# GpSimd's constants behind a norm, two transposes moved and the end of attention listed anew, in a two layer decoder trunk

## The chip, the cores and the metric

The kernel runs on one core of a Trainium2 chip. The metric is the device time of one execution in microseconds (us). The engines are TensorE (PE; its weight loads are PEld), VectorE (DVE), ScalarE (ACT), GpSimd (POOL) and SyncE (SP), which here only issues DMAs. They have queues of their own and wait for each other through semaphores.

## What is computed

A trunk of two layers on 512 tokens of 1024 channels, all in float32. Layer 0 mixes tokens by pooling, layer 1 by stick-breaking attention with 16 heads of 64, and each is followed by a squared-ReLU MLP with 4096 hidden channels. Each mixer and each MLP stands between two RMSNorms.

```python
def rms_norm(x, g):
    y = x * lax.rsqrt(jnp.mean(x * x, axis=-1, keepdims=True) + EPS)
    return y * g

for layer in range(2):
    h = rms_norm(x, mix_pre_g[layer])
    if layer < 1:
        m = pool_mixer(h, pool_w[layer], pool_scale[layer])
    else:
        q = jnp.matmul(h, w_q[0]).reshape(B, S, N_HEADS, HEAD_DIM).transpose(0, 2, 1, 3)
        o = stick_breaking_attention(q, k, v)
        m = jnp.matmul(o.transpose(0, 2, 1, 3).reshape(B, S, HD), w_o[0])
    x = x + rms_norm(m, mix_post_g[layer])
    h = rms_norm(x, mlp_pre_g[layer])
    x = x + rms_norm(sq_relu_mlp(h, w_up[layer], w_down[layer]), mlp_post_g[layer])
    if layer == 0:
        kv = jnp.matmul(rms_norm(x, kv_norm_g), w_kv)   # split into k and v, 16 heads each
```

Attention weighs key s for query t (s < t) by sigmoid(z_ts) times the product of 1 - sigmoid(z_tj) over the keys j between them; no softmax is taken.

## The kernel before, in words

Tokens stand in four tiles of 128 (t = 0 to 3), channels in two halves of 512 (n or h = 0, 1) or in eight blocks of 128 (k). For float32 accuracy each operand of a product is split into a rounded high part (a copy on ScalarE) and the rest, the low part (a subtraction on VectorE), and each product is three matmuls: high x high, high x low, low x high (`mm3`, L299, and `up_block`, L691). `up_block` serves the MLP's up projections and attention's key and query projections; with half of the tokens it is 8 x 3 = 24 matmuls of 256 columns.

**What one norm is.** `Update` (L312) carries a tile through "add the normed mixer or MLP output to x, then norm x for the next stage". Its steps, with the letters that the written orders use for them:

- `s`: two ScalarE passes sum the squares of the halves of y into columns of a small tile `stat` (`square_sum`, L284).
- `g`: VectorE multiplies y by the gain row (`product`, L332).
- `V`: GpSimd adds the two sums and eps (`total`, L289) and raises the result to -0.5 (`power`, L296). All totals and powers are on GpSimd, one column each.
- `a`: VectorE adds y times that factor to x (`add_part`, L344).
- `S`: ScalarE sums the squares of the new x. `W`: a second total and power on GpSimd.
- `n`: ScalarE scales x by the new factor (L373), half by half.
- `t`: TensorE transposes a half, four matmuls against a unit matrix (L383). `h` and `l`: ScalarE copies the high part out of PSUM (L393, or L397 where a gain is applied column by column), VectorE takes the low part (L402, L406). Together they write `xnh` and `xnl`, the operands of the next projections.

So V, a, S, W, n, t, h, l is a chain over four engines for each tile, and the four tiles' chains lie side by side.

**What sets the order.** Most of the kernel is ordered by a planner: it simulates the engines and places each instruction in its engine's queue where it expects it to be ready. Inside `tc.manual_schedule(engines=...)` the named engines keep the program's order instead, and other instructions may still be put between. `tc.issue_after(i)` places what a block issues behind instruction i in the same queue, without waiting for its result. The ends of the stages are written out by hand as lists of words.

**Attention's start.** Layer 0's MLP ends in `finish` (L438), whose list `MLP_ORDER[0]` orders TensorE, ScalarE, VectorE and GpSimd by hand up to the norms of tile 3 (n30 n31). The transposes of tiles 2 and 3 are left over as `pending`; `need(t)` (L419) issues them with their high and low parts when something first wants them. Then attention follows `ATT_ORDER` (L59). `V001` is the first value projection (4 heads) for tiles 0 and 1 (`values`, L862; 48 matmuls of 256 columns), `K0` the first half, over tiles 0 and 1, of pair 0's key projection (`start`, L884), `V02` the values of tile 2, `P0` the rest of the key projection and the query projection of pair 0 (`queries_keys`, L910). `S` are scores, sigmoids and the scan of a pair, `T` transposes of its weights, `A` their products with the values, `O` output projections. In before, tile 2's transposes come when V02 asks for them. GpSimd prepares attention's constants where the program opens attention: zeros in the unused halves of `kls` (L908), `begin` (a memset L937 and four selects L942, which mark where a row's scan begins) and single columns of `us` (L948). No order ties them to the norms.

**Attention's end.** `END_ORDER` (L72) lists the last pair's work, the last output projections (`O`, `E`, `F`, `G`, with the matmuls of L300 to L302), the four tiles' norms, and the first four up projections of layer 1's MLP over tiles 0 and 1: `R` loads up weight j, `i` and `k` split it (`high_up`, L1153, on ScalarE; `low_up`, L1157, on VectorE), `u` is its `up_block` (`half_up`, L1159). TensorE, ScalarE, VectorE, GpSimd and SP keep the list's order. The planner may put the MLP's own loads and splits between (L160, L170, L172). At the end of the list in before, VectorE does a20 l10 a21 ev30 k2 g31 g30 a31 a30 k3 l20 l21 l31 l30; ScalarE S20 i2 S21 s30 n20 n21 i3 S31 S30 h20 n31 n30 h21 h31 h30; TensorE u0 u1 t20 t21 u2 t31 t30 u3; GpSimd W2 V3 W3. After that the MLP takes the other half of the tokens (tiles 2 and 3) of the same up projections.

Of the kernel before, what the change touches and what calls it, by code (L numbers as in the profile page):

```python
# [57 lines left out]

ATT_ORDER = [  # L59
    (w[0], int(w[1]), [int(c) for c in w[2:]])  # L60
    for w in """V001 K0 V02 P0 V03 S0 P1 T0 V101 S1 A0 P2 T1 V123 A1 S2 P3 T2 O00123 A2 S3 P4 V201 T3 A3
    S4 P5 T4 V223 S5 A4 P6 V301 T5 S6 A5 V323 P7 T6 E1""".split()
]

# [15 lines left out]
    s21 t10 G31 h10 g21 V2 E30 ev31 a20 s31 F30 l10 S20 G30 a21 i2 u0 ev30 S21 k2 s30 W2 g31 V3 n20 g30  # L80
    u1 n21 a31 i3 a30 S31 k3 t20 S30 t21 h20 u2 W3 n31 l20 n30 h21 t31 t30 h31 l21 u3 h30 l31 l30""".split()
]


# [21 lines left out]
def trunk(ctx, tc, x, consts, grow, pw, wup, wdn, wq, wk, wv, wo, out):  # L106
# [12 lines left out]
    def name(s):  # L119
        uid[0] += 1  # L120
        return f"{s}{uid[0]}"
# [162 lines left out]
    def square_sum(src, junk, st, col):  # L284
        latest["act"] = nc.scalar.activation(junk, src, ACT.Square, scale=D**-0.5, accum_out=st[:, col : col + 1])  # L285

    def total(st, col, eps, op=ALU.add):

        nc.gpsimd.tensor_scalar(  # L289
            out=st[:, col + 2 : col + 3], in0=st[:, col : col + 1], scalar1=st[:, col + 1 : col + 2],  # L290
            scalar2=eps, op0=ALU.add, op1=op,
        )

    def power(st, col):
        r = st[:, col + 3 : col + 4]
        latest["pool"] = nc.gpsimd.tensor_tensor(out=r, in0=st[:, col + 2 : col + 3], in1=mhalf, op=ALU.pow)  # L296
        return r
# [14 lines left out]
    class Update:  # L312
        def __init__(self, t, gpost, scaled, eps=EPS, gpre=None, final=False, xn=None, gcol=None):

            self.t, self.gpost, self.scaled, self.eps = t, gpost, scaled, eps
            self.gpre, self.gcol, self.final = gpre, gcol, final
            self.xn = xn_tile() if xn is None else xn
            self.st = keep.tile([P, 8], F32, tag=f"stat{t}", bufs=4, name=name("stat"))


            self.cuts = NS
            if final and t == T - 1:
                self.cuts, self.scaled = [NS[0], slice(512, 768), slice(768, 1024)], xn_tile()
# [5 lines left out]

        def product(self, n, y):  # L330
            cut = self.cuts[n]
            nc.vector.tensor_tensor(out=self.scaled[:, cut], in0=y, in1=self.gpost[:, cut], op=ALU.mult)  # L332

        def first_rstd(self):
            if len(self.cuts) == 2:
                total(self.st, 0, self.eps)
            else:
                both = self.st[:, 2:3]
                nc.gpsimd.tensor_tensor(out=both, in0=both, in1=self.st[:, 4:5], op=ALU.add)
            self.r = power(self.st, 0)  # L340

        def add_part(self, n):
# [6 lines left out]
            cut = self.cuts[n]  # L349
            square_sum(xt[self.t][:, cut], self.xn[:, cut], self.st, 4 + n)  # L350

        def rstd(self):
            normed_by[self.t] = self
            if self.gpre is None and self.gcol is None:
                total(self.st, 4, EPS)
            else:

                total(self.st, 4, TINY, ALU.max)  # L360
            self.r = power(self.st, 4)

        def homogeneous_eps(self):
# [55 lines left out]
    def need(*tiles):  # L419
        for t in tiles:  # L420
            if t in pending:
                pending.pop(t).transpose()
# [265 lines left out]
        fill(ahead)  # L688
        finish(l, squares[1:], w, y, lambda t, y: update(t, y, gpost))

    def up_block(pu, w, cols):  # L691
        wh = w[0].rearrange("p (k c) -> p k c", k=KC)
        wl = w[1].rearrange("p (k c) -> p k c", k=KC)
        for k in range(KC):
            nc.tensor.matmul(pu[:, cols], wh[:, k, :], xnh[:, k, cols], start=k == 0, stop=False)  # L695
            nc.tensor.matmul(pu[:, cols], wh[:, k, :], xnl[:, k, cols], start=False, stop=False)  # L696
            nc.tensor.matmul(pu[:, cols], wl[:, k, :], xnh[:, k, cols], start=False, stop=k == KC - 1)  # L697


    with tc.tile_pool(name="mix0", bufs=1, reuse_waits="tile") as mp:  # L700
# [158 lines left out]
    with tc.tile_pool(name="att", bufs=1, reuse_waits="tile") as ap:  # L859
        att_pool[0] = ap  # L860

        def values(u, part):  # L862
            if u not in vs:
                w = [get(("v", u, h)) for h in range(2)]
                vs[u] = w, ap.tile([P, T, 4, 2, HD], F32R, tag="v", bufs=2, name=name("v"))
            w, v = vs[u]
            for s in part:
                need(s)
                pv = ps()
                for k in range(KC):  # L870
# [6 lines left out]
                nc.scalar.copy(v[:, s, :, 0, :], pv4)  # L877
                nc.vector.tensor_tensor(
                    out=v[:, s, :, 1, :], in0=pv4, in1=v[:, s, :, 0, :].bitcast(F32), op=ALU.subtract
                )  # L880
# [53 lines left out]


        begin = ap.tile([P, NSEG], mybir.dt.bfloat16, tag="begin", name="begin")
        nc.gpsimd.memset(begin, 0.0)  # L937
        us = [ap.tile([P, NSEG + 1], F32, tag=f"u{a}", name=f"u{a}") for a in range(2)]
        for lo, n in SEG.values():
            c = min(n - P, 1)  # L940
            d = begin[:, lo + n - P - c : lo + n]
            nc.gpsimd.affine_select(  # L942
                out=d, in_=d, pattern=[[-1, P + c]], base=c - 1, channel_multiplier=1,
                compare_op=ALU.not_equal, fill=1.0,
            )
        for at in [lo for lo, n in SEG.values()] + [NSEG]:
            for u in us:
                nc.gpsimd.memset(u[:, at : at + 1], 0.0)  # L948

        class Head:  # L950

# [135 lines left out]
        def end():  # L1087
# [4 lines left out]
            bank, o, ups, up = {}, {}, {}, {}  # L1092

            def projected(key, t, n, pairs, first, stop):
                if first:
# [59 lines left out]
            def low_up(j):  # L1155
                raw, (hi, lo) = up[j]
                latest["dve"] = nc.vector.tensor_tensor(out=lo, in0=raw, in1=hi.bitcast(F32), op=ALU.subtract)  # L1157

            def half_up(j):  # L1159
                early.append((ps(), up[j][1]))  # L1160
                up_block(*early[j], slice(0, S // 2))

            last_heads = heads[last]
            steps = {
# [10 lines left out]
                "g": lambda t, n: ups[t].product(n, y[t][:, NS[n]]),  # L1175
                "V": lambda t: ups[t].first_rstd(), "a": lambda t, n: ups[t].add_part(n),
# [12 lines left out]
            while key not in made:  # L1189
                make()  # L1190

        qk, heads = {}, {}
        for what, i, part in ATT_ORDER:
            if what == "V":
                values(i, part)
            elif what == "K":
                start(("k", i))
            elif what == "P":
                qk[i] = queries_keys(i)
                if i == PAIRS - 1:  # L1200
                    until(("o", 5))
            elif what == "S":
                gate[0] = True
                heads[i] = weights(i)
                fill()
            elif what == "T":
                transposed(heads[i])
                behind.update(latest)
            elif what == "A":
                mix_pair(i, vs[i // 2][1])  # L1210
            elif what == "O" and part:
                out_proj(i, part)
                if i == 0:
                    with tc.issue_after(latest["sp"].ins):
                        gpost1 = gain_row(R_MIX_POST1)
            elif what == "E":
                end()


    with tc.tile_pool(name="mlp1", bufs=1, reuse_waits="tile") as mp:  # L1220
# [55 lines left out]
```

## Time and profile before

| | |
|---|---|
| median of 3 runs | 954.42 us (954.37 to 954.46) |
| the profiled execution | 953.63 us, span 951.9 us, granted clock 0.997 |
| VectorE, ScalarE, GpSimd busy | 707.5, 576.9, 45.5 us |
| DMA | 156.15 MB, mean 164 GB/s |

The span runs from the first to the last instruction of one profiled execution; its own time is somewhat longer. A row of a timeline gives the start in us from the span's start, the length in us, the engine, the line of the kernel, the operation, output<-input and shape, the count, and in brackets how long the engine was idle before and what ended that. Rows of neighbouring equal instructions are merged. The ends of matmuls are modelled, their starts are measured, so times between TensorE's instructions are best taken from start to start. A row of a table by stretch gives the stretch, its length, the busy time of TensorE, its weight loads, VectorE, ScalarE and GpSimd with the number of instructions, the granted clock, the share of the DMA engines and GB/s.

### The profile page before, as it was taken

To read this page: it belongs to the slowest core of one execution; us is meant where nothing else is said; L and a number is where in the kernel's file an instruction comes from. 1 tells how busy PE (TensorE), PEld (TensorE's weight loads), DVE (VectorE), ACT (ScalarE), POOL (GpSimd) and SP (SyncE) were. 2 spreads that over 40 slices of the span, in tenths; PEclk is the share of its full clock that TensorE was granted. 3 is DMA by queue.
4 is the path that set the end of the run, shared out by engine and by line. 5 is a ranking of instruction groups with operands and counts; after the bars stand their busy time and mean duration, and the time that the engine had idled before them with its cause. 6 is when DMAs were issued, how large, how long until landed. Compare 5 with 4: busy or idle time off the path is not lost.

```text
span 951.9 us, 12511 instructions
## 1 busy us (share of the span) xinstructions
PE 940.5 (99%) x4758; PEld 799.6 (84%) x4758; DVE 707.5 (74%) x810; ACT 576.9 (61%) x1015; POOL 45.5 (5%) x88
## 2 busy tenths in 40 slices
PE   9999999999999999999999999999999999999996
PEld 7998888888888888899899988888888888888885
DVE  5875799988979876576577778875595966957856
ACT  6668979788775646456656554775545444444632
POOL 2300000000000014000000001300000000000002
PEclk9999999999999999999999999999999999999998
DMA  8344959789697850522424261432513233133102
GB/s 315 100 167 155 340 213 362 290 285 344 221 322 270 293 176 2 201 91 87 171 94 178 95 259 45 156 126 76 198 37 131 99 133 111 45 133 111 38 8 88
DMA packets 43263, 156.15 MB, mean 164 GB/s; under 512 B 4290, under 2 KB 4674, under 8 KB 43203
## 3 DMA queue, kind: packets, MB, share of 16 engines
q1 hardware_dynamic: 43202, 155.36, 46.3%
q8 instruction: 37, 0.61, 0.3%
q14 instruction: 24, 0.19, 0.1%
HBM read 121.79 MB, written 33.55 MB: 163 GB/s over the span
## 4 chain that ended last, share of the span: by engine, by line
PE 93%; ACT 2%; POOL 1%; DVE 1%; issue 1%; DMA 1%; SPq 0%; POOLq 0%; DVEq 0%; ACTq 0%
PE ps L577 28%; PE ps L697 15%; PE ps L695 15%; PE ps L696 15%; PE ps L300 4%; PE ps L302 4%; PE ps L301 4%; PE ps L1030 2%; PE ps L1013 2%; PE ps L809 1%; PE ps L969 1%; ACT xn L285 1%; PE ps L970 1%; PE ps L383 1%; POOL stat L289 1%
## 5 line engine op out<-in xcount | busy, mean ns | idle before, releaser
L577 PE MATMUL ps<-w,a 128*128 128x512 f32 x1176 | 278.6, 389 | 0.0
L697 PE MATMUL ps<-xnh,w 128*128 128x512 f32 (+1 forms) x712 | 261.5, 368 | 0.1
L696 PE MATMUL ps<-xnl,w 128*128 128x512 f32 (+1 forms) x712 | 261.3, 368 | 0.0
L695 PE MATMUL ps<-xnh,w 128*128 128x512 f32 (+1 forms) x712 | 261.2, 368 | 0.0
L577 PEld LDWEIGHTS ps<-w,a 128*128 128x128 f32 x1176 | 220.6, 188 | 45.9 <-DVE w L282 0.2
L697 PEld LDWEIGHTS ps<-xnh,w 128*128 128x128 f32 x712 | 134.1, 188 | 22.5 <-DVE w L830 0.3
L696 PEld LDWEIGHTS ps<-xnl,w 128*128 128x128 f32 x712 | 134.2, 189 | 21.8
L695 PEld LDWEIGHTS ps<-xnh,w 128*128 128x128 f32 x712 | 133.7, 189 | 22.0
L586 DVE TENSOR_TENSOR y<-ps,y 128x512 f32<-128x512 f32 x124 | 84.4, 687 | 42.7 <-PE ps L577 42.6
L172 DVE TENSOR_TENSOR w<-raw,w 128x1024 fp32r<-128x1024 f32 x58 | 70.9, 1222 | 56.7 <-ACT w L170 56.5
L170 ACT CAST w<-raw 128x1024 fp32r<-128x1024 f32 x58 | 61.0, 1051 | 78.0 <-PE ps L697 77.8
L281 ACT CAST a<-r 128x768 fp32r<-128x768 f32 (+1 forms) x60 | 47.6, 794 | 73.4 <-PE ps L577 54.5
L282 DVE TENSOR_TENSOR a<-r,a 128x768 fp32r<-128x768 f32 (+1 forms) x60 | 54.1, 901 | 12.4 <-ACT a L281 12.2
L281 ACT CAST w<-e 128x1536 fp32r<-128x1536 f32 (+1 forms) x30 | 41.8, 1395 | 26.0 <-DVE e L551 16.6
L994 DVE TENSOR_TENSOR_SCAN e<-u,begin 128x1280 f32<-128x1280 f32 x16 | 45.2, 2822 | 10.9 <-ACT u L978 10.4
L282 DVE TENSOR_TENSOR w<-e,w 128x1536 fp32r<-128x1536 f32 (+1 forms) x30 | 49.4, 1647 | 1.8 <-ACT w L281 1.6
L181 ACT ACTIVATE apart<-apart,eye 128x128 f32<-128x128 f32 (+1 forms) x132 | 43.1, 407 | 0.0
L282 DVE TENSOR_TENSOR w<-w,w 128x1536 fp32r<-128x1536 f32 (+1 forms) x20 | 33.0, 1650 | 7.9 <-ACT w L281 7.9
L609 ACT ACTIVATE r<-ps 128x512 f32<-128x512 f32 x56 | 33.0, 590 | 8.9 <-PE ps L697 8.9
L300 PE MATMUL ps<-w,xnh 128*128 128x256 f32 x128 | 36.5, 286 | 0.9 <-ACT xnh L393 0.9
L282 DVE TENSOR_TENSOR w<-xn,w 128x1536 fp32r<-128x1536 f32 (+1 forms) x20 | 33.0, 1650 | 5.6 <-ACT w L281 5.5
L610 ACT ACTIVATE r<-r 128x512 f32<-128x512 f32 x56 | 35.5, 634 | 1.3
(133 smaller groups left out, 1395.9 us busy)
## 6 DMA issues: line engine op xcount, KB each, us to landing
raw<-in_wup SPq DMA_DIRECT2D x64, 512.0 KB, 4.2
w<-kept SPq DMA_DIRECT2D x60, 512.0 KB, 4.2
kept<-wx SPq DMA_DIRECT2D x30, 512.0 KB, 4.9
w<-in_wdn SPq DMA_DIRECT2D x8, 1536.0 KB, 6.7
kept<-apart SPq DMA_DIRECT2D x24, 512.0 KB, 5.8
xn<-in_wdn SPq DMA_DIRECT2D x8, 1536.0 KB, 8.3
apart<-in_wk SPq DMA_DIRECT2D x7, 512.0 KB, 7.1
apart<-in_wq SPq DMA_DIRECT2D x7, 512.0 KB, 9.3
```

Source lines behind the costliest of these rows:

```text
L170: nc.scalar.copy(hi, raw)
L172: nc.vector.tensor_tensor(out=lo, in0=raw, in1=hi.bitcast(F32), op=ALU.subtract)
L181: nc.scalar.mul(c, c, gc[:, lo + k : lo + k + 1])
L281: latest["act"] = nc.scalar.copy(hi, src)
L282: latest["dve"] = nc.vector.tensor_tensor(out=lo, in0=src, in1=hi.bitcast(F32), op=ALU.subtract)
L300: nc.tensor.matmul(dst, ah, bh, start=start, stop=False)
L577: nc.tensor.matmul(bank, a[:, x, q, TS[t]], w[:, z, q], start=start and q == 0 and k == 0, stop=q == self.n - 1 and k == 2, skip_group_che ...
L586: nc.vector.tensor_tensor(out=part, in0=bank, in1=part, op=ALU.add)
L695: nc.tensor.matmul(pu[:, cols], wh[:, k, :], xnh[:, k, cols], start=k == 0, stop=False)
L696: nc.tensor.matmul(pu[:, cols], wh[:, k, :], xnl[:, k, cols], start=False, stop=False)
L697: nc.tensor.matmul(pu[:, cols], wl[:, k, :], xnh[:, k, cols], start=False, stop=k == KC - 1)
L994: nc.vector.tensor_tensor_scan(out=self.e[:, ::-1], data0=self.u[:, 1:][:, ::-1], data1=begin[:, ::-1], initial=0.0, op0=ALU.mult, op1=ALU ...
```

## The change

1. GpSimd's constants (`kls`, `begin`, `us`) are issued behind the latest power on GpSimd, the one of the last tile's norm.
2. `ATT_ORDER` gets two words: `N2` issues tile 2's transposes ahead of K0, `N3` tile 3's behind it and ahead of V02. TensorE keeps the program's order from V001 to P0.
3. `END_ORDER` from k2 on is listed anew. Tile 2's second total (`wt2`), tile 3's first (`vt3`) and tile 3's second (`wt3`) run on VectorE instead of GpSimd; the powers stay on GpSimd. `H` remembers the latest power, and VectorE's next g, a or k waits until it is done. VectorE's order becomes a20 l10 a21 ev30 wt2 (H) g31 g30 vt3 (H) a31 a30 k2 wt3 l20 k3 (H) l21 l31 l30, where (H) stands at what waits. k2 thus goes from before the products to behind the addition, k3 from before l20 to behind it. The orders of ScalarE and TensorE in the list stay as they were.
4. `up_block` for u2 does the 16 matmuls with the weight's high part first, and then the 8 with its low part.

The number of instructions on TensorE and of DMAs is the same. The rest of the diff moves code into functions.

```diff
 ATT_ORDER
-    V001 K0 V02 P0 V03 S0 P1 ...
+    V001 N2 K0 N3 V02 P0 V03 S0 P1 ...
 END_ORDER
-    ... S20 G30 a21 i2 u0 ev30 S21 k2 s30 W2 g31 V3 n20 g30
-    u1 n21 a31 i3 a30 S31 k3 t20 S30 t21 h20 u2 W3 n31 l20 n30 h21 t31 t30 h31 l21 u3 h30 l31 l30
+    ... S20 G30 a21 i2 u0 ev30 S21 s30 wt2 W2 H g31 g30 vt3 n20 V3 H
+    u1 n21 a31 i3 a30 k2 S31 t20 S30 t21 wt3 W3 H h20 u2 l20 n31 k3 n30 h21 t31 t30 h31 l21 u3 h30 l31 l30
...
-    def total(st, col, eps, op=ALU.add):
-        nc.gpsimd.tensor_scalar(
+    def total(st, col, eps, op=ALU.add, engine=None):
+        (engine or nc.gpsimd).tensor_scalar(
...
-    def up_block(pu, w, cols):
+    def up_block(pu, w, cols, last=False):
+        def low(k):
+            nc.tensor.matmul(pu[:, cols], wl[:, k, :], xnh[:, k, cols], start=False, stop=k == KC - 1)
         for k in range(KC):
             nc.tensor.matmul(pu[:, cols], wh[:, k, :], xnh[:, k, cols], start=k == 0, stop=False)
             nc.tensor.matmul(pu[:, cols], wh[:, k, :], xnl[:, k, cols], start=False, stop=False)
-            nc.tensor.matmul(pu[:, cols], wl[:, k, :], xnh[:, k, cols], start=False, stop=k == KC - 1)
+            if not last:
+                low(k)
+        if last:
+            for k in range(KC):
+                low(k)
...
-        for a in range(2):
-            nc.gpsimd.memset(kls[a][half[1 - a], :].bitcast(F32), 0.0)
+        with tc.issue_after(latest["pool"].ins):
+            for a in range(2):
+                nc.gpsimd.memset(kls[a][half[1 - a], :].bitcast(F32), 0.0)
...
+        with tc.issue_after(latest["pool"].ins):
+            nc.gpsimd.memset(begin, 0.0)
...
+            def hold():
+                held.append(latest["pool"].ins)
+
+            def released(i):
+                if held:
+                    info = mybir.DependencyInfo(mybir.DependencyClass.Sync, mybir.DependencyReason.DATA)
+                    tc.add_manual_dep(i.ins, held.pop().name, info, reason="port")
...
+                "g": lambda t, n: released(ups[t].product(n, y[t][:, NS[n]])), "H": hold,
+                "vt": lambda t: ups[t].first_total(nc.vector), "wt": lambda t: ups[t].second_total(nc.vector),
...
+            elif what == "N":
+                need(i)
...
+        first = [what for what, _, _ in ATT_ORDER].index("P") + 1
+        with tc.manual_schedule(engines={mybir.EngineType.PE}):
+            for x in ATT_ORDER[:first]:
+                step(*x)
+        for x in ATT_ORDER[first:-1]:
+            step(*x)
+        end()
```

More of the change, by code (lines that the diff above doesn't have):

```diff
@@ L60 @@
     (w[0], int(w[1]), [int(c) for c in w[2:]])
-    for w in """V001 K0 V02 P0 V03 S0 P1 T0 V101 S1 A0 P2 T1 V123 A1 S2 P3 T2 O00123 A2 S3 P4 V201 T3 A3
+    for w in """V001 N2 K0 N3 V02 P0 V03 S0 P1 T0 V101 S1 A0 P2 T1 V123 A1 S2 P3 T2 O00123 A2 S3 P4 V201 T3 A3
     S4 P5 T4 V223 S5 A4 P6 V301 T5 S6 A5 V323 P7 T6 E1""".split()
@@ L79 @@
     l01 F20 S10 k1 G20 i0 W1 E21 ev20 R3 n11 k0 s20 F21 t11 h00 g20 G21 R2 E31 h11 l00 ev21 F31 n10 l11
-    s21 t10 G31 h10 g21 V2 E30 ev31 a20 s31 F30 l10 S20 G30 a21 i2 u0 ev30 S21 k2 s30 W2 g31 V3 n20 g30
-    u1 n21 a31 i3 a30 S31 k3 t20 S30 t21 h20 u2 W3 n31 l20 n30 h21 t31 t30 h31 l21 u3 h30 l31 l30""".split()
+    s21 t10 G31 h10 g21 V2 E30 ev31 a20 s31 F30 l10 S20 G30 a21 i2 u0 ev30 S21 s30 wt2 W2 H g31 g30 vt3 n20 V3 H
+    u1 n21 a31 i3 a30 k2 S31 t20 S30 t21 wt3 W3 H h20 u2 l20 n31 k3 n30 h21 t31 t30 h31 l21 u3 h30 l31 l30""".split()
 ]
@@ L331, in product, with first_total @@
             cut = self.cuts[n]
-            nc.vector.tensor_tensor(out=self.scaled[:, cut], in0=y, in1=self.gpost[:, cut], op=ALU.mult)
+            return nc.vector.tensor_tensor(out=self.scaled[:, cut], in0=y, in1=self.gpost[:, cut], op=ALU.mult)
+        def first_total(self, engine=None):
+            total(self.st, 0, self.eps, engine=engine)
+            self.summed = True
         def first_rstd(self):
             if len(self.cuts) == 2:
-                total(self.st, 0, self.eps)
+                if not self.summed:
+                    self.first_total()
             else:
@@ L350, in squares_of_x, with second_total @@
             square_sum(xt[self.t][:, cut], self.xn[:, cut], self.st, 4 + n)
+        def second_total(self, engine=None):
+            if self.gpre is None and self.gcol is None:
+                total(self.st, 4, EPS, engine=engine)
+            else:
+                total(self.st, 4, TINY, ALU.max, engine=engine)
+            self.summed = True
         def rstd(self):
             normed_by[self.t] = self
[L354 to L360, printed above, removed]
+            if not self.summed:
+                self.second_total()
             self.r = power(self.st, 4)
@@ L936, in trunk @@
         begin = ap.tile([P, NSEG], mybir.dt.bfloat16, tag="begin", name="begin")
-        nc.gpsimd.memset(begin, 0.0)
         us = [ap.tile([P, NSEG + 1], F32, tag=f"u{a}", name=f"u{a}") for a in range(2)]
[L939 to L948, printed above, removed]
+        with tc.issue_after(latest["pool"].ins):
+            nc.gpsimd.memset(begin, 0.0)
+            for lo, n in SEG.values():
+                c = min(n - P, 1)
+                d = begin[:, lo + n - P - c : lo + n]
+                nc.gpsimd.affine_select(
+                    out=d, in_=d, pattern=[[-1, P + c]], base=c - 1, channel_multiplier=1,
+                    compare_op=ALU.not_equal, fill=1.0,
+                )
+            for at in [lo for lo, n in SEG.values()] + [NSEG]:
+                for u in us:
+                    nc.gpsimd.memset(u[:, at : at + 1], 0.0)
         class Head:
@@ L1190, in until, with step @@
                 make()
-        qk, heads = {}, {}
-        for what, i, part in ATT_ORDER:
+        qk, heads, gpost1 = {}, {}, None
+        def step(what, i, part):
+            nonlocal gpost1
             if what == "V":
                 values(i, part)
+            elif what == "N":
+                need(i)
             elif what == "K":
```

12 lines of the change are left out of this document (6 added, 6 removed).

## The prediction

> **What bounds the kernel now.** I read the views in this order: spans, busy times, TensorE's own waits, stretches, and then the timeline of each engine around the two places that the diff edits. The span of the only core, and TensorE's share of it:
>
> ```profile
> core 0: 951.9 us, clock 0.997
> ```
> ```profile
> PE 940.5 (99%) x4758; PEld 799.6 (84%) x4758; DVE 707.5 (74%) x810; ACT 576.9 (61%) x1015; POOL 45.5 (5%) x88
> ```
>
> TensorE is busy for 99% at a granted clock of 0.997. The diff leaves the number of matmuls as it is, so it can only win time in which TensorE stands still. The list of its waits (total, times, longest; waits at the kernel's first instructions stand above these rows and are not touched) is short:
>
> ```profile
> PE ps L383 <- ACT xn L373: 1.3, 2, 1.1
> PE ps L300 <- ACT xnh L393: 0.9, 1, 0.9
> PE ps L969 <- DVE q L926: 0.4, 1, 0.4
> ```
>
> L383 is a transpose that waits for ScalarE's normed rows (L373); L300 is a value projection that waits for the high part of a transposed tile (L393). The middle of attention has nothing to give: by the stretches, it idles 195.00 - 194.54 = 0.46 us in 385 to 580, but 0.94 us in the 18 us before.
>
> ```profile
> 367.00:385.00 18.00, 17.06 (x139) 16.67 (x138) 8.90 (x15) 8.68 (x20) 6.59 (x23) 1.00 0.01 2
> 385.00:580.00 195.00, 194.54 (x1156) 172.94 (x1155) 135.11 (x146) 113.50 (x250) 0.00 (x0) 1.00 0.40 146
> ```
>
> **First place: attention's start.** TensorE's timeline (start, length, line; tiles are counted from 0 as in the code):
>
> ```profile
> 376.30 1.04 PE L383 MATMUL ps<-eye,xn 128*128 128x128 f32 x8
> 378.28 0.38 PE L300 MATMUL ps<-w,xnh 128*128 128x256 f32 x1 [0.94 <-ACT xnh L393]
> 378.50 0.28 PE L301 MATMUL ps<-w,xnh 128*128 128x256 f32 x1
> 378.62 1.04 PE L383 MATMUL ps<-eye,xn 128*128 128x128 f32 x8
> 379.41 0.36 PE L302 MATMUL ps<-w,xnl 128*128 128x256 f32 x1
> ```
>
> The second transposes (tile 3) take 379.41 - 378.62 = 0.79 us until the next matmul starts; the first ones (tile 2) take 378.28 - 376.30 = 1.98. So 1.19 us are lost, more than the modelled 0.94, because ends are modelled and starts are not. A 256 column matmul follows the last after 0.12 us (378.50 to 378.62). ScalarE shows why the tile's high part is late:
>
> ```profile
> 376.42 1.33 ACT L373 ACTIVATE xn<-x,stat 128x512 f32<-128x512 f32 x2 [1.07 <-POOL stat L296]
> 377.66 0.56 ACT L393 CAST xnh<-ps 128x512 fp32r<-128x512 f32 x1
> ```
>
> It norms tile 3 first, and that waited 1.07 us for GpSimd's power (L296); the high part of tile 2 comes at 377.66, directly behind. GpSimd's timeline has attention's constants between the total and the power of tile 2:
>
> ```profile
> 368.88 0.30 POOL L289 TENSOR_SCALAR stat<-stat 128x1 f32<-128x1 f32 x1
> 369.24 0.40 POOL L948 MEMSET u<- 128x1 f32 x10
> 369.59 1.69 POOL L942 TENSOR_SCALAR_AFFINE_SELECT begin<-begin 128x129 bf16<-128x129 bf16 x3
> 371.25 0.56 POOL L296 TENSOR_TENSOR stat<-stat,mhalf 128x1 f32<-128x1 f32 x1
> ```
>
> **What the edits do there.** N2 puts tile 2's transposes ahead of the key projection's first half (K0), N3 tile 3's behind it, and TensorE keeps that order up to P0. Then tile 2's high part has 24 matmuls of 0.12 = 2.88 us of cover in place of none. V001 ends, in the new order, at 376.30 - 2.88 = 373.4. Are the normed rows there? The power ends at 371.25 + 0.56 = 371.8, and two normings take 1.33: 373.1 even with the constants in the way, about 2 us earlier without. So N2 starts without a wait, lasts 0.79, K0 ends at 373.4 + 0.8 + 2.9 = 377.1, and N3 comes then. In before tile 3's normed rows are complete at 376.42 + 1.33 = 377.75. If nothing else moved, the second four transposes would wait some 0.3 us. Moving the constants takes that away too, as far as VectorE's timeline allows:
>
> ```profile
> 369.68 1.44 DVE L332 TENSOR_TENSOR y<-y,grow 128x512 f32<-128x512 f32 x2
> 371.51 0.42 DVE L878 TENSOR_TENSOR v<-ps,v 128x256 fp32r<-128x256 f32 x1 [0.39 <-ACT v L877]
> 372.99 1.42 DVE L344 SCALAR_TENSOR_TENSOR x<-y,stat,x 128x512 f32<-128x512 f32 x2 [1.05 <-POOL stat L296]
> ```
>
> Tile 3's addition (L344) waits 1.05 us for its power; without the constants it starts behind L878 at 371.9, so its norm can come about 1 us earlier, ahead of 377.1. But the planner may put the copy of the second values ahead of the squares on ScalarE; then the 0.3 stays. Gain here: 0.9 to 1.2, I take **1.1**. The constants themselves now start behind tile 3's power. GpSimd's whole busy time in 367 to 385 is 6.59, totals included, so even from 376.4 they end by 383. Their first reader is the first scan, which comes after P0, and GpSimd's 0.00 busy in 385 to 580 says that nothing queues behind them: I cost their move at nothing, with P0 as cover.
>
> **Second place: attention's end.** TensorE's timeline there:
>
> ```profile
> 619.96 0.28 PE L697 MATMUL ps<-xnh,w 128*128 128x256 f32 x1
> 621.37 1.27 PE L383 MATMUL ps<-eye,xn 128*128 128x128 f32 x8 [1.14 <-ACT xn L373]
> 622.39 0.36 PE L695 MATMUL ps<-xnh,w 128*128 128x256 f32 x1
> ```
>
> The last matmul of u2 frees TensorE at 619.96 + 0.12 = 620.08; tile 3's transposes start at 621.37 and hand on at 622.39, 1.02 later where 0.79 is undisturbed. Lost: 1.29 + 0.23 = **1.52 us**, the most that this place can give. VectorE and GpSimd around tile 2's second total:
>
> ```profile
> 611.97 1.22 DVE L1157 TENSOR_TENSOR w<-raw,w 128x1024 fp32r<-128x1024 f32 x1
> 613.11 1.28 DVE L332 TENSOR_TENSOR y<-y,grow 128x512 f32<-128x512 f32 x2
> 616.27 1.42 DVE L344 SCALAR_TENSOR_TENSOR x<-y,stat,x 128x512 f32<-128x512 f32 x2 [1.88 <-POOL stat L296]
> ```
> ```profile
> 612.37 2.19 POOL L289 TENSOR_SCALAR stat<-stat 128x1 f32<-128x1 f32 x1 [3.40 <-ACT xn L285]
> ...
> 618.84 0.30 POOL L289 TENSOR_SCALAR stat<-stat 128x1 f32<-128x1 f32 x1 [2.60 <-ACT xn L285]
> 619.22 0.56 POOL L296 TENSOR_TENSOR stat<-stat,mhalf 128x1 f32<-128x1 f32 x1
> ```
>
> The total, 0.30 elsewhere, takes 2.19 and ends at 614.56, right after VectorE's run of k2 and two products (613.11 + 1.28 = 614.39). A GpSimd instruction that reads the statistics stands still while VectorE reads two operands from SBUF. The rest is ScalarE's queue (the first row ends tile 2's squares, the second tile 3's):
>
> ```profile
> 612.09 0.19 ACT L285 ACTIVATION_READ_ACCUMULATOR xn<-x 128x1 f32 x1
> ...
> 618.56 0.18 ACT L285 ACTIVATION_READ_ACCUMULATOR xn<-x 128x1 f32 x1
> 618.65 1.03 ACT L170 CAST dn<-dn 128x1024 fp32r<-128x1024 f32 x1
> 619.59 1.12 ACT L397 ACTIVATE xnh<-ps,eye 128x128 fp32r<-128x128 f32 x4
> 620.60 0.72 ACT L373 ACTIVATE xn<-x,stat 128x512 f32<-128x512 f32 x1
> ```
>
> **What the edits do there.** A one column total on VectorE is bounded by a row from the MLP:
>
> ```profile
> L366 DVE TENSOR_SCALAR stat<-stat 128x1 f32<-128x1 f32 x8 | 1.2, 206 | 0.0
> ```
>
> From the end of tile 2's squares, 612.28: total 0.21, power 0.56, two handovers at 0.1 (my estimate from 618.56 + 0.18 to the total and 618.84 + 0.38 to the power): 613.2. The products wait for that power (H), at 613.3 to 614.6, about as long as k2 kept them before; queued behind them on VectorE are vt3, the addition and k2, and ScalarE's squares wait for the addition. vt3 and its power: 615.5. Addition 615.5 to 616.9, against 616.27 to 617.69: 0.8 earlier. Squares follow on ScalarE, where the norm of tile 2 and i3 (a cast of L170's size) are done by 613.3 + 1.33 + 1.03 = 615.7: end at about 617.7 against 618.74. k2, moved behind the addition, holds VectorE to 618.1; wt3 then 0.2, power until 618.9 against 619.22 + 0.56 = 619.78. The moved k2 is needed by the low products of u2. These now come last; u2 starts at 620.08 - 2.88 = 617.2, so from 617.2 + 16 x 0.12 = 619.1: 1.0 us of cover, and in the old order TensorE would have stood for 618.1 - 617.4 = 0.7 us. k3 (1.22) now stands behind wt3's power and l20, which follows L397 by a quarter of its 1.12: it ends near 620.4 or, with L170 ahead of L397, 621.2; u3's third matmul wants it at 621.1 or 621.6, cover of 0.4 at least. None of the moved steps issues a DMA, and SP's queue keeps its order.
>
> ScalarE decides the rest. L170 (1.03) is not in the written order; the planner puts it where it expects a gap. Where it stays, ahead of L397, tile 3's norm starts at 617.7 + 0.95 + 1.05 = 619.7, halves at 620.35 and 621.0, and u3 starts near 621.4 against 622.39: gain 0.95. Where it moves away, the norm starts at 618.95, TensorE has no wait, and the gain is 1.5. I take **1.2**, between the ends, since the trace cannot say which.
>
> Sum: 1.1 + 1.2 = 2.3 us. The profiled execution took 953.63 (span 951.9); it would take 951.3. The median of the timed runs is 954.42, 0.8 above the profiled one, and the same subtraction gives **952.1**. With the bounds (0.9 + 0.95 to 1.2 + 1.5) the forecast's own range is 951.7 to 952.6.
>
> **The rivals.**
> (1) *The last norm stays late.* L172, the Vector half of L170's pair, isn't held. If it lands right behind wt3, its 1.22 stops the power, which then ends near 620.2, and u3 starts near 622.0: gain 0.4 there, 0.9 to 1.1 at the first place, so 952.9; 952.6 to 953.8 with variants. For it: the pair already lies in this gap. Against: in before it lies behind k3, not between total and power. These two rows, one of each engine, say that coming first doesn't protect GpSimd:
>
> ```profile
> 607.46 0.86 POOL L289 TENSOR_SCALAR stat<-stat 128x1 f32<-128x1 f32 x1 [5.01 <-ACT xn L285]
> ```
> ```profile
> 607.55 0.69 DVE L332 TENSOR_TENSOR y<-y,grow 128x512 f32<-128x512 f32 x1
> ```
>
> The total started 0.09 us before the product, yet it took 0.86 and the product its usual 0.69. The Trainium skill (SBUF — State Buffer, Who interferes with whom) says that a Vector instruction with two SBUF inputs contends with a GpSimd instruction that reads SBUF, which the 2.19 row bears out, and that whichever issues first keeps the port for its whole length. By that second rule a power that starts ahead of L172 would lose nothing and rival 1 would come out at the forecast; the rows at 607.46 and 607.55 speak against it.
> (2) *The middle of attention is planned anew and loses.* Behind P0 the planner sets TensorE's order by its own clock. The place is the scores' wait for the split queries (0.4 us once, PE ps L969). It decides where VectorE's split of a pair ends after TensorE arrives at its scores. At 0.4 in each of seven pairs, 2.8 us are lost, 0.5 more than is won: 954.9, slower than before. Slower by over 0.2% takes 4.2 us, waits of 0.6 per pair. Against: only one such wait in before, and edits that only advance the start.
> (3) *More than forecast.* Both places give all, 2.7, and the 0.4 at the scores goes: 951.3.
> (4) *It doesn't do what it says.* TensorE's order is fixed by hand at both places, and the 1.19 us disappear with K0 as cover, so I give this no chance of its own beyond (1).
>
> **How the numbers follow.** Forecast 0.55, rival 1 0.24, rival 2 0.14, rival 3 0.07. The range 951.4 to 954.4 leaves out most of rival 2 and half of rival 3, about 0.16. About 0.2% (1.9 us) is what a measurement of this kernel can tell from no change: below 952.5 lie 0.50 of the forecast and rival 3, 0.57; above 956.3 half of rival 2, 0.07; the rest is 0.36.
>
> **What would show it.** Right: tile 2's transposes before the key projection and hand-on within 0.8; GpSimd's totals and powers at 0.30 and 0.56 around 368 and 613 to 619; the constants after the last power; tile 3's last transposes behind u2 with under 0.5 us of wait. Wrong: a wait at L383 for L373 at 377 or 620, a power of over 1 us near 618, a wait at L697 for L1157 (k2 or k3 late), or more than 0.5 us idle on TensorE in the middle of attention.

## The result and the profile after

| | before | after |
|---|---|---|
| median of 11 runs | 954.34 us | 952.16 us |
| lowest and highest | 953.93, 954.46 | 951.4, 952.63 |
| the profiled execution, its span | 953.63, 951.9 us | 952.24, 950.5 us |

The ratio is 0.9978, 95% interval [0.9968, 0.9987]: 2.2 us faster. The spans differ by 1.4 us only. In the profiled execution of after, the stages ahead of attention, which no edit touches, ran 0.79 us later (V001's first matmul at 368.46 against 367.67). So the two places are compared by their own stretches, start to start on TensorE. Counted from V001's first matmul to the kernel's last matmul, which leaves those stages out, it is 944.28 - 367.67 = 576.61 us in before and 942.98 - 368.46 = 574.52 in after: 2.09 us less.

The list of TensorE's waits of after (total, times, longest), behind the one at the kernel's start:

```profile
PE ps L395 <- ACT xn L385: 0.5, 2, 0.3
PE ps L991 <- DVE q L947: 0.4, 1, 0.4
```

The wait for ScalarE's high part (L393 in before, L405 now) is gone. The one for normed rows (L383, now L395) went from 1.3 to 0.5 us. The table by stretch has, for the middle of attention:

```profile
385.00:580.00 195.00, 194.55 (x1154) 172.86 (x1153) 135.48 (x147) 113.83 (x251) 0.00 (x0) 1.00 0.40 146
```

0.45 us idle against 0.46: nothing was won or lost there.

**First place.** TensorE's timeline of after:

```profile
374.21 1.04 PE L395 MATMUL ps<-eye,xn 128*128 128x128 f32 x8
375.00 0.36 PE L711 MATMUL ps<-xnh,w 128*128 128x256 f32 x1
...
377.95 1.04 PE L395 MATMUL ps<-eye,xn 128*128 128x128 f32 x8
378.74 0.36 PE L300 MATMUL ps<-w,xnh 128*128 128x256 f32 x1
```

Both tiles' transposes hand on after 0.79 us. The 1.19 us of before are gone. GpSimd's and ScalarE's timelines show why neither tile is late:

```profile
368.78 0.30 POOL L289 TENSOR_SCALAR stat<-stat 128x1 f32<-128x1 f32 x1 [4.29 <-ACT xn L285]
369.17 0.56 POOL L296 TENSOR_TENSOR stat<-stat,mhalf 128x1 f32<-128x1 f32 x1
370.22 0.37 POOL L289 TENSOR_SCALAR stat<-stat,eps 128x1 f32<-128x1 f32 x1 [0.49 <-ACT xn L285]
370.67 0.89 POOL L296 TENSOR_TENSOR stat<-stat,mhalf 128x1 f32<-128x1 f32 x1
...
374.70 0.56 POOL L296 TENSOR_TENSOR stat<-stat,mhalf 128x1 f32<-128x1 f32 x1
375.32 1.09 POOL L929 MEMSET kl<- 64x512 f32 x2
```
```profile
374.85 1.08 ACT L405 CAST xnh<-ps 128x512 fp32r<-128x512 f32 x2
375.81 1.34 ACT L385 ACTIVATE xn<-x,stat 128x512 f32<-128x512 f32 x2
```

The first two rows are tile 2's second total and power, the next two tile 3's first. Tile 2's power now follows its total at once; the constants run from 375.32, behind tile 3's second power (374.70). Tile 2's high part (L405) comes while TensorE does K0, and tile 3's norm is complete at 377.15, 0.8 us ahead of its transposes.

**Second place.** TensorE, from the end of u2 to u3:

```profile
618.61 1.12 PE L708 MATMUL ps<-xnh,w 128*128 128x256 f32 x8
620.05 1.27 PE L395 MATMUL ps<-eye,xn 128*128 128x128 f32 x8 [0.32 <-ACT xn L385]
621.08 0.36 PE L711 MATMUL ps<-xnh,w 128*128 128x256 f32 x1
```

u2's eight low products (the matmuls with the weight's low part) now stand in one row at its end. They free TensorE at 618.61 + 8 x 0.12 = 619.57. The transposes start 0.48 later and take 1.03 in place of 0.79. Left standing: 0.72 of the 1.52 us; won: 0.80. From the start of tile 2's transposes to u3 it is 621.08 - 615.83 = 5.25 us (in before 622.39 - 616.33 = 6.06). VectorE, GpSimd and ScalarE there:

```profile
612.70 1.29 DVE L333 TENSOR_TENSOR y<-y,grow 128x512 f32<-128x512 f32 x2 [0.66 <-POOL stat L296]
613.91 0.21 DVE L289 TENSOR_SCALAR stat<-stat 128x1 f32<-128x1 f32 x1
614.78 1.42 DVE L351 SCALAR_TENSOR_TENSOR x<-y,stat,x 128x512 f32<-128x512 f32 x2 [0.67 <-POOL stat L296]
616.12 1.22 DVE L1189 TENSOR_TENSOR w<-raw,w 128x1024 fp32r<-128x1024 f32 x1
617.26 1.23 DVE L172 TENSOR_TENSOR dn<-dn,dn 128x1024 fp32r<-128x1024 f32 x1
618.41 0.21 DVE L289 TENSOR_SCALAR stat<-stat 128x1 f32<-128x1 f32 x1
```
```profile
612.12 0.55 POOL L296 TENSOR_TENSOR stat<-stat,mhalf 128x1 f32<-128x1 f32 x1 [3.63 <-DVE stat L289]
614.20 0.55 POOL L296 TENSOR_TENSOR stat<-stat,mhalf 128x1 f32<-128x1 f32 x1 [1.53 <-DVE stat L289]
618.69 0.55 POOL L296 TENSOR_TENSOR stat<-stat,mhalf 128x1 f32<-128x1 f32 x1 [3.94 <-DVE stat L289]
```
```profile
616.20 1.03 ACT L170 CAST dn<-dn 128x1024 fp32r<-128x1024 f32 x1
617.14 0.63 ACT L285 ACTIVATE xn<-x 128x512 f32<-128x512 f32 x1
```

No power is stalled (0.55 each), and VectorE stands 0.66 us twice, waiting for one. The planner put the pair of the MLP's own split elsewhere than before: ScalarE's half (L170) between tile 3's two sums of squares, VectorE's (L172) right ahead of wt3.

### The profile page after: what moved, and what is told of

Read it like the earlier page. It is cut to its first block, busy times and chain, and to the rows that moved or that the text cites. A ratio compares the mean times of both kernels' runs of the same rounds, so it can differ in the third digit from the quotient of the medians.

```text
span 950.5 us, 12510 instructions
## 1 busy us (share of the span) xinstructions
PE 940.9 (99%) x4758; PEld 799.7 (84%) x4758; DVE 707.9 (74%) x813; ACT 577.8 (61%) x1015; POOL 42.1 (4%) x85
## 4 chain that ended last, share of the span: by engine, by line
PE 94%; DVE 2%; ACT 2%; POOL 1%; issue 1%; POOLq 0%; DVEq 0%; ACTq 0%
PE ps L589 28%; PE ps L708 15%; PE ps L712 15%; PE ps L711 15%; PE ps L300 4%; PE ps L301 4%; PE ps L302 4%; PE ps L1052 2%; PE ps L829 1%; PE ps L1035 1%; PE ps L991 1%; PE ps L395 1%; PE ps L992 1%; ACT xn L285 1%; PE ps L801 1%
## 5 line engine op out<-in xcount | busy, mean ns | idle before, releaser
L172 DVE TENSOR_TENSOR w<-raw,w 128x1024 fp32r<-128x1024 f32 x58 | 70.9, 1223 | 57.4 <-ACT w L170 57.2
L170 ACT CAST w<-raw 128x1024 fp32r<-128x1024 f32 x58 | 61.0, 1051 | 79.3 <-PE ps L708 79.2
```

Of the source, the lines that this page charges most:

```text
L170: nc.scalar.copy(hi, raw)
```

## The experiments

The theory (theory A): TensorE's standing time at the two places is all that the change can win; at the first it is tile 2's high part behind tile 3's norm on ScalarE, at the second tile 3's norm. The rivals are named with each kernel. All were timed in five rounds beside the kernel before; its medians in the three groups were 954.18, 954.14 and 954.29 us. Line numbers are those of each kernel.

**e1_constants**: the kernel before, with only the constants moved.

```diff
+        with tc.issue_after(latest["pool"].ins):
             # kls, begin and us
```

> The kernel before with one edit: GpSimd's constants of attention go behind the last power. TensorE's order at attention's start stays as before (tile 2's transposes behind the key projection's first half). Theory A (TensorE stands still for tile 2's high part, which stands behind tile 3's norm on ScalarE): tile 3's norm comes about 1 us earlier, so the 1.19 us that follow tile 2's transposes shrink to 0.3 to 0.5 even without the new order; 0.7 to 0.9 us faster than before, the end as before. Rival B (only the order counts, the constants were hidden): the gap stays at about 1.2 and the time does not move.

953.62 us, ratio 0.9993 [0.9984, 1.0002]. TensorE:

```profile
377.20 1.04 PE L383 MATMUL ps<-eye,xn 128*128 128x128 f32 x8
378.48 0.39 PE L300 MATMUL ps<-w,xnh 128*128 128x256 f32 x1 [0.24 <-ACT xnh L393]
```

From the start of tile 2's transposes to the next matmul it went from 1.98 to 1.28 us: 0.70 won without the new order, as theory A says. Rival B falls. The 0.49 us that stay above 0.79 are no longer ScalarE's queue, for ScalarE now stands ready and waits for the transposes:

```profile
377.84 1.07 ACT L393 CAST xnh<-ps 128x512 fp32r<-128x512 f32 x2 [1.43 <-PE ps L383]
```

They are the time of the high part itself, for which TensorE has no other work in its order here. The time alone (0.6 us, an interval that reaches 1) would not settle it; the trace does.

**e2_order**: the kernel before, with only the order.

```diff
-    V001 K0 V02 P0 V03 ...
+    V001 N2 K0 N3 V02 P0 V03 ...
```

> The kernel before with one edit: tile 2's transposes ahead of K0 and tile 3's behind it, TensorE in program order up to P0; the constants stay between the powers, the end as before. Theory A: the gap behind tile 2's transposes goes, tile 3's second four transposes wait about 0.3 to 0.5 us for the late norm; 0.7 to 0.9 us faster. Rival B (only the order counts): the full 1.2 us. Rival C (each edit needs the other): under 0.3 us.

954.17 us, ratio 0.9998 [0.9989, 1.0007]: nothing. Theory A's number was wrong here and rival C's came out. ScalarE, and TensorE's transposes of tile 3:

```profile
375.04 0.59 ACT L405 CAST xnh<-ps 128x512 fp32r<-128x512 f32 x1
375.52 0.63 ACT L285 ACTIVATE xn<-x 128x512 f32<-128x512 f32 x1
...
378.42 1.33 ACT L385 ACTIVATE xn<-x,stat 128x512 f32<-128x512 f32 x2 [1.07 <-POOL stat L296]
```
```profile
379.19 1.27 PE L395 MATMUL ps<-eye,xn 128*128 128x128 f32 x8 [0.89 <-ACT xn L385]
```

Tile 2's high part, now early, goes between tile 3's squares (375.04, and the second half at 376.14), and delays its norm to 378.42: 9.77 us after V001's first matmul (368.65), in before 376.42 - 367.67 = 8.75. TensorE's last key product ahead of them starts at 378.02, so it is free at 378.02 + 0.12 = 378.14. It waits 1.05 us at tile 3's transposes, which then take 1.03 until the next start in place of 0.79: 1.29 us lost in place of 1.19. The wait has only moved. The two edits need each other: the constants bring 0.7, the order brings the last 0.5 only with them.

**e3_end**: the kernel before, with the end's edits alone.

> The kernel before with the end's edits alone (three totals on VectorE, H, k2 and k3 moved, u2's low products last); attention's start as before. Theory A: the two places are independent, so this gains what the changed kernel gains at the end, 0.8 us, from tile 2's last transposes to the start of u3, and the start keeps its 1.2 us gap. Rival: the end's gain depends on what the planner did after the new start; then the stretch from the transposes to u3 differs from the changed kernel's 5.25 us by over 0.3.

953.18 us, ratio 0.999 [0.9982, 0.9999].

```profile
616.48 1.03 PE L395 MATMUL ps<-eye,xn 128*128 128x128 f32 x8
...
620.69 1.27 PE L395 MATMUL ps<-eye,xn 128*128 128x128 f32 x8 [0.30 <-ACT xn L385]
621.71 0.37 PE L711 MATMUL ps<-xnh,w 128*128 128x256 f32 x1
```

The stretch is 5.23 us, the changed kernel's 5.25, and the first place keeps its wait (0.9 for L405). So the end's gain does not hang on the new start.

**e4_pair_behind**: the changed kernel, with the MLP's own splits issued behind the end.

```diff
                 for step, which in END_ORDER:
                     steps[step](*which)
+            behind.update(latest)
```

> The changed kernel with one edit: the MLP's own splits (L170 and L172, the pair dn among them) are issued behind the end's last steps on ScalarE and VectorE. Theory A (the 0.7 us that TensorE still stands before u3 are the pair's, which holds up tile 3's squares on ScalarE and its total on VectorE): the stretch from tile 2's last transposes to u3 falls from 5.25 to about 4.6 us, and the time by 0.6 to 0.7 us against the changed kernel. Rival D (the handovers between VectorE and GpSimd set the rest): the stretch falls by under 0.2 us. Rival E: the pair costs the same behind the end, where TensorE then waits for a low part of the up weights: the stretch falls, the total time doesn't.

951.08 us, ratio 0.9967 [0.9955, 0.998].

```profile
615.38 1.03 PE L395 MATMUL ps<-eye,xn 128*128 128x128 f32 x8
...
619.13 1.03 PE L395 MATMUL ps<-eye,xn 128*128 128x128 f32 x8
619.92 0.36 PE L711 MATMUL ps<-xnh,w 128*128 128x256 f32 x1
```

The stretch is 4.54 us, 0.71 shorter, and no wait is left at the last transposes. The rest was the pair's; rivals D and E fall. The time is 1.1 us under the changed kernel's 952.16, which was taken in another group, and 0.6 to 0.7 was expected. From V001's first matmul to the last one it is 0.66 us shorter, so the traces give the edit no more than that. L170 and L172 were moved together; what each costs alone was not run.

**e5_no_hold**: the changed kernel without H.

```diff
             def hold():
-                held.append(latest["pool"].ins)
+                pass
```

> The changed kernel without H: the products, the addition and k3 do not wait for GpSimd's powers (nothing else changes; the results are the same). Theory F (H trades a stalled power for a standing VectorE and wins little): the power of tile 2's second norm takes about 1.0 us in place of 0.55 beside the product, VectorE no longer stands 0.66 us before the products, and tile 3's addition starts up to 0.5 us earlier; the stretch from tile 2's last transposes to u3 stays within 0.3 of 5.25 us and the time within 0.3 us of the changed kernel. Rival G (H is what brings the end's gain): a power of over 1.2 us, the stretch at 5.7 or more, 0.5 us or more slower.

951.52 us, ratio 0.9975 [0.9965, 0.9984]. GpSimd's power beside the two products of VectorE:

```profile
611.79 0.93 POOL L296 TENSOR_TENSOR stat<-stat,mhalf 128x1 f32<-128x1 f32 x1 [3.62 <-DVE stat L289]
613.11 0.55 POOL L296 TENSOR_TENSOR stat<-stat,mhalf 128x1 f32<-128x1 f32 x1 [0.40 <-DVE stat L289]
```
```profile
611.63 1.28 DVE L333 TENSOR_TENSOR y<-y,grow 128x512 f32<-128x512 f32 x2
```

The power takes 0.93, not over 1.2, and u3 does not start later: rival G falls. The stretch is 4.54, which neither theory expected, because the planner now put L170 behind tile 3's squares (616.17) and L172 behind wt3. There L172 pushes k3 (L1189), which ends at 619.41 + 1.22 = 620.63, and u3's third matmul stands for it:

```profile
620.26 0.28 PE L712 MATMUL ps<-xnl,w 128*128 128x256 f32 x1
620.68 0.39 PE L708 MATMUL ps<-xnh,w 128*128 128x256 f32 x1
```

It could have started at 620.26 + 0.12 = 620.38. So 0.30 of the 0.71 us are lost again, behind the end of the stretch. This kernel changes two things; e9 separates them.

**e6_totals_gpsimd**: the changed kernel, its three totals back on GpSimd.

```diff
-"vt": ... first_total(nc.vector), "wt": ... second_total(nc.vector)
+"vt": ... first_total(), "wt": ... second_total()
```

> The changed kernel with its three moved totals back on GpSimd, H and the order kept. Theory F: tile 2's second total, with VectorE empty beside it, takes 0.30 and costs as much as 0.21 plus a handover; tile 3's first total runs into the two products and ends behind them, as vt3 did; tile 3's second total meets L172 and ends behind it, as wt3 did. The stretch from tile 2's last transposes to u3 stays within 0.3 of 5.25 us. Rival H (VectorE's totals bring the gain): a total of 1 to 2 us again, the stretch at 5.7 or more.

951.99 us, ratio 0.9978 [0.9969, 0.9987], the changed kernel's.

```profile
610.84 0.30 POOL L289 TENSOR_SCALAR stat<-stat 128x1 f32<-128x1 f32 x1 [3.40 <-ACT xn L285]
611.22 0.56 POOL L296 TENSOR_TENSOR stat<-stat,mhalf 128x1 f32<-128x1 f32 x1
611.88 1.32 POOL L289 TENSOR_SCALAR stat<-stat 128x1 f32<-128x1 f32 x1
```
```profile
611.82 1.29 DVE L333 TENSOR_TENSOR y<-y,grow 128x512 f32<-128x512 f32 x2 [1.28 <-POOL stat L296]
```

With VectorE empty the total takes 0.30. The next one, beside the products, takes 1.32 and ends 0.09 us behind them, where vt3 would have started anyway. The stretch is 4.94 us, 0.31 shorter where at most 0.3 either way was expected, but u3 then stands for k3:

```profile
620.52 0.39 PE L708 MATMUL ps<-xnh,w 128*128 128x256 f32 x1 [0.28 <-DVE w L1189]
```

It could have started at 620.09, so 0.43 us are lost there, and in all nothing is won. Here too the planner put the pair elsewhere (L170 behind tile 3's squares, at 616.01), so the stretch does not compare the totals alone. The end of tile 3's squares does, since it lies ahead of the pair, as in e4: 1.29 us after the start of tile 2's last transposes, in e4 1.16. Rival H falls: where the totals run matters little (0.13 us) once VectorE is kept empty beside the first.

**e7_low_in_place_pair_behind**: e4, with u2's low products back in their places.

```diff
-                up_block(*early[j], slice(0, S // 2), j == 2)
+                up_block(*early[j], slice(0, S // 2))
```

> The changed kernel with the MLP's own splits behind the end (as in e4_pair_behind) and u2's low products back in their old places, every third matmul. Theory A: k2 ends 0.5 us behind u2's third matmul, so TensorE waits there for L1189 about 0.5 us and the time is 0.3 to 0.5 us above e4_pair_behind. Rival: k2 is early enough, no wait, the time of e4_pair_behind.

951.89 us, ratio 0.9976 [0.9967, 0.9985], 0.8 above e4 of the other group.

```profile
616.87 0.38 PE L708 MATMUL ps<-xnh,w 128*128 128x256 f32 x1 [0.24 <-DVE w L1189]
```

u2's third matmul starts at 616.87, where 616.35 (the start of the one ahead of it) + 0.12 = 616.47 was possible: 0.40 us late. From tile 2's transposes to tile 3's it is 619.61 - 615.35 = 4.26 us against e4's 619.13 - 615.38 = 3.75: 0.51 longer, as expected. So moving k2 costs half a microsecond unless the low products come last. That this is hidden in the changed kernel itself, where TensorE waits for tile 3 behind u2 anyway, is argued from the rows above and was not run.

**e8_first_hold**: e4, with an H behind W0.

```diff
-... s10 W0 g11 O30
+... s10 W0 H g11 O30
```

> e4_pair_behind with one more H behind W0, so that tile 1's product g11 waits for the power of tile 0's second norm (in the changed kernel that power runs beside VectorE's products and takes 0.9 in place of 0.56 us, and TensorE waits for tile 0's normed rows near 595). Theory A: the power takes 0.56, the norm comes 0.35 us earlier, and TensorE's 0.56 us around tile 0's transposes fall to 0.2; 0.3 us faster than e4_pair_behind. Rival: what g11 loses comes back as a later first factor of tile 1, and the time stays.

950.63 us, ratio 0.9968 [0.9955, 0.998]. TensorE at tile 0's transposes:

```profile
595.08 1.23 PE L395 MATMUL ps<-eye,xn 128*128 128x128 f32 x8
596.07 0.48 PE L300 MATMUL ps<-w,ohl 128*128 128x512 f32 x1
```

They start without a wait and hand on after 0.99. In after they start 0.33 us late (595.57, where 595.01 + 0.23 was possible) and take 1.02:

```profile
595.57 1.27 PE L395 MATMUL ps<-eye,xn 128*128 128x128 f32 x8 [0.16 <-ACT xn L385]
596.59 0.48 PE L300 MATMUL ps<-w,ohl 128*128 128x512 f32 x1
```

So 0.36 us are won, as expected.

**r_after, e10_first_hold, e9_only_first_hold**: one group, the changed kernel again, e8 again, and e8 with no H but the first.

> The changed kernel once more, on the chip of the next two kernels, to compare them with it directly: 952.0 to 952.3 us, the stretch from tile 2's last transposes to u3 at 5.25 us.

> The kernel of e8_first_hold once more (the MLP's own splits behind the end, one more H behind W0). By the stretches of its trace it is 0.71 us faster than the changed kernel at the last place and 0.36 at tile 0's transposes: 1.1 us under the changed kernel of this call, 951.0. Rival: the 1.5 us between the medians of the two calls hold; or the difference is the chip's, and the two come out alike.

> As e10_first_hold, but H only behind W0: the products and additions of tiles 2 and 3 and k3 do not wait for the powers; all orders are the same. Theory F (there H costs the chain 0.4 us and wins nothing): tile 3's squares end about 0.75 us behind the start of tile 2's last transposes, in place of 1.16, the power beside a product takes 0.9 us; TensorE waits in neither kernel, so the time is that of e10_first_hold within 0.3 us. Rival G (H protects the power): tile 3's squares end later than with H, and u3 starts later.

| | median | ratio to before | tile 2's transposes to u3 |
|---|---|---|---|
| r_after | 952.25 us | 0.998 [0.9971, 0.9989] | 5.22 us |
| e10_first_hold | 951.11 us | 0.9969 [0.9956, 0.9981] | 4.54 us |
| e9_only_first_hold | 950.87 us | 0.9967 [0.9954, 0.9979] | 4.54 us |

e10 lies 1.1 us under the changed kernel, as its stretches say; the 1.5 us between the groups was too much. In e9 tile 3's squares end 0.80 us after tile 2's last transposes start, in e10 1.23: H costs the last tile's chain 0.4 us there, and the power beside a product still takes 0.93. TensorE waits in neither, so the times agree within 0.3. e9 is 1.4 us under the changed kernel of the same group; that it is faster than e10 is not shown (0.24 us, and their runs overlap).

Because the groups differ by some tenths, here is the stretch from V001's first matmul to the kernel's last one, from each profiled execution. It leaves out the stages ahead, which no edit touches:

| | from, to | us | less than before |
|---|---|---|---|
| before | 367.67, 944.28 | 576.61 | |
| after | 368.46, 942.98 | 574.52 | 2.09 |
| r_after | 368.51, 943.05 | 574.54 | 2.07 |
| e1_constants | 368.57, 944.45 | 575.88 | 0.73 |
| e2_order | 368.65, 945.28 | 576.63 | -0.02 |
| e3_end | 367.88, 943.61 | 575.73 | 0.88 |
| e4_pair_behind | 367.95, 941.81 | 573.86 | 2.75 |
| e5_no_hold | 368.12, 942.36 | 574.24 | 2.37 |
| e6_totals_gpsimd | 367.42, 942.20 | 574.78 | 1.83 |
| e7_low_in_place_pair_behind | 367.95, 942.28 | 574.33 | 2.28 |
| e8_first_hold | 368.28, 941.82 | 573.54 | 3.07 |
| e10_first_hold | 368.78, 942.38 | 573.60 | 3.01 |
| e9_only_first_hold | 368.21, 941.75 | 573.54 | 3.07 |

The two pairs of equal kernels agree within 0.06 us here, and the differences are those of the places within some 0.15: 0.66 from after to e4 (0.71 by the stretch), 0.47 lost from e4 to e7 (0.51), 0.32 won from e4 to e8 (0.36), 0.28 from after to e5 (0.71 - 0.30).

## Why the prediction was right, point by point

- *TensorE's standing time bounds the gain*: right. 952.1 was predicted, 952.16 measured; that it came so near is luck in part, as the two places show. The middle of attention stayed at 0.45 us idle, so rival 2 did not happen, and rival 3 neither.
- *First place, 1.1 us (0.9 to 1.2)*: right, all 1.19 came. One step of it failed: with the constants in the way I put what stays at 0.3 us ("If nothing else moved, the second four transposes would wait some 0.3 us"). e2 measured 1.29. I had moved the transposes but not what follows them: the high part, once early, takes ScalarE's time from tile 3's squares. And the constants cost tile 3's norm more than the 1 us that I put: counted from V001's first matmul it starts at 6.50 us in e1 (375.07 - 368.57), in before at 8.75.
- *Second place, 1.2 us (0.95 to 1.5)*: the mechanism was right, the size was not: 0.80. The mis-sized term is L170 and L172. I priced L170 ahead of L397 or away. The planner chose a third place, between tile 3's squares and ahead of wt3, and there the pair costs 0.71 us (e4). That is near rival 1, but through VectorE's own queue: L172 made wt3 wait, no power was stalled there. The prediction named a wait at 620 among the signs of being wrong and one of under 0.5 us among those of being right; it is there, with 0.48 us.
- *Handovers*: right. From the end of tile 2's squares (611.61 + 0.19) to the end of the power (612.12 + 0.55) it is 0.87 us; the sum had 613.2 - 612.28 = 0.9.
- *What relieves the total of 2.19 us*: I followed the edits as they stand and gave the totals on VectorE and H no prices of their own. e6 shows that the totals can stay, e5 and e9 that H can go. One of the two is enough, since each keeps tile 2's second total clear of the products. From the start of tile 2's last transposes to the end of tile 3's squares it is 2.41 us in before, 1.29 with H alone (e6), 1.16 with both (e4) and 0.75 with VectorE's totals alone (e5): H costs the chain 0.4 us. k2 at its old place, with the rest of the change, was not tried, so how much of this its move alone brings is open.
- *k2 has cover by the low products*: right, and worth 0.5 us without the pair (e7); the prediction had 0.7.
- *GpSimd's totals and powers beside VectorE's products*: 0.30 and 0.56 were forecast around 368. Tile 3's first total and power took 0.37 and 0.89 there (370.22, 370.67), beside the two products, and TensorE did not wait for them. The Trainium skill (SBUF — State Buffer, Who interferes with whom) has a Vector instruction with two SBUF inputs contend with a GpSimd instruction that reads SBUF. The trace agrees: 0.93 and 1.32 us beside the products, 0.55 and 0.30 with VectorE empty. The traces do not bear out the other thing that the prediction took from there, that whichever issues first keeps the port: the total that it quoted started 0.09 us ahead and took 0.86. The one at 370.22 starts 0.24 us ahead of its products and takes 0.37, but at its usual 0.30 it would have been nearly done by then, so it says little.

The sum was near by two errors that offset: 0.1 too little at the first place, 0.4 too much at the second, and the medians show 0.2 us more than the places explain (2.2 against 2.0). In the traces it is 0.1 (2.09), which lies between the two places: behind u3's start, both kernels take 321.9 us to the last matmul. That rest is within what the medians of equal kernels differ by (952.16 and 952.25 for the changed kernel, 950.63 and 951.11 for e8), and I do not explain it.

## What to carry to other kernels

Where one engine is busy for 99%, take its waits one by one, from start to start, and add only those. An edit of the order on one engine moves the waits of the others: follow the instruction that becomes early as well as the one that becomes late (e2 gained nothing, and the same edit with the constants moved gained 0.5 us more than the constants alone). Work that no written order holds lands in the gaps of a written one; tie it behind (0.7 us here), and try each protective wait by itself, since the same H was worth 0.36 us at tile 0, and at tiles 2 and 3 it cost the chain 0.4 us and won nothing. And read on behind the place: in e5 and e6 what a stretch won was lost again, in part or whole, at u3's third matmul.

## What the runs showed of the hardware

Beside two products in a row, each 0.68 us, GpSimd's power and its total behave differently. In e5 the power starts 0.16 us after the first product and ends at 612.72, about 0.4 us after the first product's end (611.63 + 0.68) and before the second's (612.91). In e6 the total starts 0.06 us after the first and ends at 613.20, 0.09 behind the second (613.11). The 2.19 us total of before likewise outlasted three instructions. So the power was done ahead of the second product's end, and the total was not. Beside a single product (593.66 in the changed kernel, 0.68 us) the power at 593.84 took 0.92, as long as beside two. Why the two differ was not tried.
